# The first layer's MLP in two passes: the context, then the latents in units with seven products for eight

## The chip, the core and the metric

One core of a Trainium2 chip runs the whole kernel. The time is device microseconds (us) of one execution; the metric is the median over runs. TensorE (PE) does the matrix products and has a queue for weight loads of its own (PEld). VectorE (DVE), ScalarE (ACT) and GpSimd (POOL) do the elementwise work, and SyncE (SP) issues the DMA transfers.

## The reference, cut to what matters

```python
def _mlp(h, w1, w2):                       # D_MODEL 1024, hidden 4096
    return jnp.square(jax.nn.relu(h @ w1)) @ w2

for i in range(2):                         # layer 0: conv/Fourier mixer; layer 1: neighbourhood attention
    sx1, cx1, gx1, sx2, cx2, gx2 = split(cond_x @ ada_w[i] + ada_b[i])   # for the latents
    sc1, cc1, gc1, sc2, cc2, gc2 = split(cond_c @ ada_w[i] + ada_b[i])   # for the context
    x = x + gx1 * mixer_i(modulate(rms(x), sx1, cx1))                    # 1024 latent tokens
    if i == 0: ctx = ctx + gc1 * mixer_0(modulate(rms(ctx), sc1, cc1))   # 256 context tokens
    x = x + gx2 * _mlp(modulate(rms(x), sx2, cx2), w1[i], w2[i])
    if i == 0: ctx = ctx + gc2 * _mlp(modulate(rms(ctx), sc2, cc2), w1[i], w2[i])
return x
```

In layer 1 the context gives keys and values, so that `ctx` is needed for its norm and its part of K and V, and no longer after that. All data are fp32.

## The kernel before

**Tokens and numbers.** Tokens lie along the free axis, channels along the 128 partitions. They are cut into chunk 0 and chunk 1 (512 latent tokens each) and chunk 2 (256 context tokens). Every operand of a product is held as a high and a low part, and a product is three matmuls into one PSUM bank: high by high, high by low, low by high (`mm3`, lines 298 to 300). A group of matmuls ends in PSUM; `residual` (line 315, DVE) scales it by the gate and adds it to the tokens' tile `xT`, which frees the bank. There are eight banks.

**Weights.** 512 KB of weights come into a tile `raw` (three of them, tag `wraw`) by one DMA of SP's queue. Each half becomes a piece `wsp` (four of them): ACT copies the high part (line 251), and POOL, or in places DVE, subtracts to get the low part (line 252).

**Layer 0's MLP.** `mlp(0, norm, (2, 1, 0), 0, 1, end0)` walks over eight blocks of 512 hidden channels. In a block four groups of the first product (`up`: ACT line 970 relu and line 972 square, POOL line 973 square again, DVE line 974 low part) run over the chunks 2, 1 and 0 with the same weights; the second product follows in groups over the same chunks, each ended by a `residual`. So 1280 tokens share each piece of weights, and 128 pieces serve the pass.

**Work beside it.** `tick` gives places to `ada_filler`: it takes a step of layer 1's adaLN map, eight reductions on DVE (line 222, two instructions each) of a 512 KB tile. 48 steps are needed; all of them stand beside this pass. At its start chunk 0's norm stands between the products (`norm.stat`, then `norm.out` per 128 channels: lines 404 to 412 on DVE, ACT and POOL). At its end `end0` puts the squares of the next norm (line 377) behind the residuals, and chunk 0's norm ahead of the last groups.

**After it.** The products of Q, K and V (lines 1163 and 1164) take the chunks as token tiles of 128: tiles 0 to 3 are chunk 0, 4 to 7 chunk 1, 8 and 9 the context. The first weight kind begins with chunk 0, then takes the context, then chunk 1. Layer 1's MLP does part of the work here described as units (`unit_head`, `unit_tail`, `unit_down`): 256 hidden channels, 2 by 2 blocks of the first product formed with seven products of sums for eight (Strassen's way, in Winograd's form). Sums of the tokens (`token_sums`, `token_sum_3`, `token_sum_4`: lines 1383 to 1411) and of the weights (`make_s2`) are made on DVE and POOL for that.

A scheduler ahead of time decides how the instructions of one engine stand in its queue; each engine runs its queue in order. The functions of the kernel that the change touches are these.

Of the kernel before, what the change touches and what calls it, by code (L numbers as in the profile page):

```python
# [36 lines left out]
def trunk(ctx: ExitStack, tc, x_t, cx_t, vecs, cc, ada, ada_t, w_in, w_out_2, w_fold, w_32, mlp_w1, mlp_w2, w_qkv, na_w_out_2, na_w_out_4, bias_pad,  # L37
# [916 lines left out]
    gs = partial_groups(y_hi[2:4], y_lo[2:4], 0, 0, (0,), 2, done=lambda m, ci: norm.square(m, ci, POOL if m % 2 else DVE))  # L954
    close_stream(gs[:4], gs[4:], (1,), norm)


    def mlp(l, norm, cis, late, fill, end, nf=8, beside=()):


        beside = list(beside)
        hh, hl = norm.hi, norm.lo

        def up(pcs, ci, uh, ul, between=None):
            off, w, _ = CHUNKS[ci]
            ps = dense(pcs, ci, hh, hl)
            if between:
                between()
            r, q = tmp(), tmp()
            ACT.activation(r[:, :w], ps[:, :w], AF.Relu)  # L970
            hs = uh[:, off:off + w]
            ACT.activation(hs, r[:, :w], AF.Square)
            POOL.tensor_tensor(out=q[:, :w], in0=r[:, :w], in1=r[:, :w], op=ALU.mult)  # L973
            DVE.tensor_tensor(out=ul[:, off:off + w], in0=q[:, :w], in1=hs.bitcast(F32), op=ALU.subtract)  # L974

        order = [ci for ci in cis if ci != late] + [late]
        for fc in range(nf):
            uh = [big("uh") for _ in range(4)]
            ul = [big("ul") for _ in range(4)]
            f = 0  # L980
            if fc == 0:
                pcs = take()
                pcs += [w for a in plan.pop(0) for w in pieces(*a, lambda: big("wq")[:, 0:1024])]
                for n, ci in enumerate(order):
                    for i in range(3):
# [4 lines left out]
                        else:  # L990
                            up(w, ci, uh[i], ul[i])
                            if beside and (ci, i) > (late, 0):
                                beside.pop(0)()
                f = 3
            while f < 4:
                pcs = take()
                for ci in order:
                    up(pcs, ci, uh[f], ul[f])
                    if beside:
                        beside.pop(0)()  # L1000
# [695 lines left out]
```

## Time and profile before

| what | value |
|---|---|
| median of three runs | 2715.81 us (2714.42 to 2718.0) |
| the profiled execution's own time | 2716.18 us |
| its span in the trace | 2714.4 us |
| PE busy | 2631.4 us, 97% |
| DVE busy | 1682.5 us, 62% |
| ACT busy | 914.5 us, 34% |
| POOL busy | 1029.1 us, 38% |

The span is the time from the first to the last instruction that the profiler shows. Busy shares are means over stages that have different limits, so the stretches are read one by one. A matmul's busy time overlaps the next one's, so that the rate at which PE works is read from starts, or from the count of matmuls in a stretch.

### The profile page before, as it was taken

The page shows a single profiled execution, that of the slowest core. Times are in us where ns is not written, and L with a number is a line of the kernel's source. Part 1 is how long each engine was busy: PE and PEld are TensorE (multiplying, and loading weights), DVE is VectorE, ACT ScalarE, POOL GpSimd, SP SyncE. Part 2 cuts the span into 40 slices and gives each one's busy share as a digit, 9 for nine tenths or more (in the row PEclk, how much of TensorE's full clock was granted, in tenths as well). Part 3 has the DMA queues.
Part 4 walks back from the last instruction along what each step waited for, and adds up shares of the span by engine and source line. Part 5 has one row for each costly group of instructions (what it writes and reads, how often), then busy time and mean ns, then how long its engine had stood idle before and what let it go on. Part 6 is the DMA issues. An engine that isn't in the chain of part 4 may idle for free. (4 is left out here: it accounts for less than half of the span.)

```text
span 2714.4 us, 37385 instructions
## 1 busy us (share of the span) xinstructions
PE 2631.4 (97%) x13787; PEld 2186.2 (81%) x13787; DVE 1682.5 (62%) x3635; ACT 914.5 (34%) x1988; POOL 1029.1 (38%) x850
## 2 busy tenths in 40 slices
PE   7999898999999999999999999999999999999999
PEld 5878787888888888888778887788877788888887
DVE  5798678454465555623962544888879855555555
ACT  4211246121221211213532324766754232332332
POOL 3232347232332322323410102444457644544543
PEclk8999899999999999999999999999999999999999
DMA  7244320222222222311333444434321111111112
GB/s 249 72 132 130 124 75 16 68 88 82 82 94 69 86 90 78 94 47 43 101 115 107 122 130 143 148 105 143 104 59 39 47 47 47 63 47 47 63 47 86
DMA packets 150395, 239.46 MB, mean 88 GB/s; under 512 B 10892, under 2 KB 94124, under 8 KB 150212
## 3 DMA queue, kind: packets, MB, share of 16 engines
q1 hardware_dynamic: 148772, 234.45, 27.2%
q8 instruction: 109, 1.79, 0.3%
q10 hardware_dynamic: 1440, 2.62, 0.3%
q14 instruction: 74, 0.61, 0.1%
HBM read 208.71 MB, written 28.32 MB: 87 GB/s over the span
## 5 line engine op out<-in xcount | busy, mean ns | idle before, releaser
L252 POOL TENSOR_TENSOR wsp<-raw,wsp 128x512 fp32r<-128x512 f32 x355 | 498.4, 1407 | 898.6 <-ACT wsp L251 871.1
L315 DVE SCALAR_TENSOR_TENSOR xT<-ps,mods,xT 128x512 f32<-128x512 f32 x544 | 380.7, 711 | 316.8 <-PE ps L300 316.2
L298 PE MATMUL ps<-uh,wsp 128*128 128x512 f32 (+1 forms) x1280 | 471.2, 369 | 10.5 <-DVE xT L315 10.5
L299 PE MATMUL ps<-ul,wsp 128*128 128x512 f32 (+1 forms) x1280 | 471.7, 369 | 0.6 <-DVE ul L1505 0.6
L300 PE MATMUL ps<-uh,wsp 128*128 128x512 f32 (+1 forms) x1280 | 470.6, 368 | 0.0
L222 DVE CUSTOM_DVE_ANT_0 junk<-raw,cond_b 128x256 bf16<-128x256 f32 x640 | 346.3, 541 | 198.9 <-DMA raw<-in_ada_t_dram 167.3
L251 ACT CAST wsp<-raw 128x512 fp32r<-128x512 f32 x368 | 226.1, 619 | 716.2 <-PE ps L300 540.6
L299 PE MATMUL ps<-ml,wsp 128*128 128x512 f32 (+1 forms) x792 | 285.4, 361 | 9.7 <-DVE ml L412 7.5
L298 PEld LDWEIGHTS ps<-uh,wsp 128*128 128x128 f32 x1280 | 241.3, 188 | 55.1 <-DVE xT L315 10.8
L298 PE MATMUL ps<-mh,wsp 128*128 128x512 f32 (+1 forms) x792 | 283.9, 360 | 1.2 <-ACT mh L405 1.2
L300 PE MATMUL ps<-mh,wsp 128*128 128x512 f32 (+1 forms) x792 | 283.6, 359 | 0.0
L299 PEld LDWEIGHTS ps<-ul,wsp 128*128 128x128 f32 x1280 | 241.3, 189 | 41.0 <-DVE ul L1505 1.1
L300 PEld LDWEIGHTS ps<-uh,wsp 128*128 128x128 f32 x1280 | 241.0, 188 | 40.6
L973 POOL TENSOR_TENSOR tmp<-tmp 128x512 f32<-128x512 f32 (+1 forms) x104 | 103.3, 994 | 217.1 <-ACT tmp L970 148.2
L299 PEld LDWEIGHTS ps<-ml,wsp 128*128 128x128 f32 x792 | 150.9, 191 | 36.5 <-DVE ml L412 10.9
L298 PEld LDWEIGHTS ps<-mh,wsp 128*128 128x128 f32 x792 | 150.9, 191 | 24.6 <-ACT mh L405 1.4
L300 PEld LDWEIGHTS ps<-mh,wsp 128*128 128x128 f32 x792 | 151.0, 191 | 21.3
L1499 PE MATMUL ps<-mh,wsp 128*128 128x512 f32 x448 | 142.6, 389 | 0.0
L970 ACT ACTIVATE tmp<-ps 128x512 f32<-128x512 f32 (+1 forms) x104 | 55.3, 531 | 255.5 <-PE ps L300 250.8
L298 PE MATMUL ps<-hh,wsp 128*128 128x512 f32 (+1 forms) x360 | 130.1, 361 | 3.9 <-ACT wsp L251 3.6
L974 DVE TENSOR_TENSOR ul<-tmp,uh 128x512 fp32r<-128x512 f32 (+1 forms) x104 | 92.4, 893 | 66.5 <-POOL tmp L973 66.5
L299 PE MATMUL ps<-hl,wsp 128*128 128x512 f32 (+1 forms) x360 | 129.4, 359 | 2.0 <-DVE hl L412 1.4
(335 smaller groups left out, 5098.5 us busy)
## 6 DMA issues: line engine op xcount, KB each, us to landing
raw<-in_mlp_w_dram SPq DMA_DIRECT2D x96, 512.0 KB, 3.5
raw<-in_ada_t_dram SPq DMA_DIRECT2D x80, 512.0 KB, 3.8
raw<-in_mlp_w_dram SPq DMA_DIRECT2D x72, 256.0 KB, 2.7
raw<-in_w_qkv_dram SPq DMA_DIRECT2D x24, 512.0 KB, 4.1
k_d<-tmp SPq DMA_DIRECT2D x40, 256.0 KB, 2.4
kh<-k_d SPq DMA_DIRECT2D x15, 640.0 KB, 5.0
kl<-k_d SPq DMA_DIRECT2D x15, 640.0 KB, 7.3
araw<-in_ada_dram SPq DMA_DIRECT2D x16, 512.0 KB, 9.4
```

Source lines behind the costliest of these rows:

```text
L222: DVE.tensor_tensor_reduce(out=junk, in0=raw[:, d * 256:d * 256 + 256], in1=cond_b, op0=ALU.mult, op1=ALU.add, scale=1.0, scalar=0.0, accu ...
L251: ACT.copy(dst_hi, src)
L252: lo_eng.tensor_tensor(out=dst_lo, in0=src, in1=dst_hi.bitcast(F32), op=ALU.subtract)
L298: PE.matmul(ps, lhsT=whi, rhs=ahi, start=first, stop=False)
L299: PE.matmul(ps, lhsT=whi, rhs=alo, start=False, stop=False)
L300: PE.matmul(ps, lhsT=wlo, rhs=ahi, start=False, stop=last)
L315: DVE.scalar_tensor_tensor(out=xT[dt][ci], in0=ps, scalar=mods[l][:, 24 * k + 16 + dt, s:s + 1], in1=xT[dt][ci], op0=ALU.mult, op1=ALU.add)
L970: ACT.activation(r[:, :w], ps[:, :w], AF.Relu)
L973: POOL.tensor_tensor(out=q[:, :w], in0=r[:, :w], in1=r[:, :w], op=ALU.mult)
L974: DVE.tensor_tensor(out=ul[:, off:off + w], in0=q[:, :w], in1=hs.bitcast(F32), op=ALU.subtract)
L1499: PE.matmul(ps, lhsT=a, rhs=b, start=(first and kt == 0 and n == 0), stop=(kt == 3 and n == 2), skip_group_check=True)
```

## The change

Layer 0's MLP becomes two passes. The first is the context alone: 64 tiles `raw`, 128 pieces, and twelve matmuls of 256 columns with each piece. Every third piece is split on DVE, the others on POOL. Beside it stand the norms of chunks 1 and 0 and the sums of the latents (`sums_12`, `sum_3`, near the end `sum_4`). The context is then saved to DRAM and its tile is reused. The second pass is the latents: the class `Seven`, which also takes the place of layer 1's code, runs over 16 units of 256 hidden channels. The weights are so loaded and split a second time, with sums of the weights (`make_s2`) in every unit. In the first 14 units two adaLN steps stand beside the second product; the other 20 go beside Q, K and V, where none stood before. The last unit's second product goes chunk by chunk (with its weights made twice), and the first kind of QKV begins with the context's tiles 8 and 9.

```diff
-    def plan_mlp(l, n=8):
...
-    plan_mlp(0)
...
-    fillers.extend([ada_filler] * 49)
-    mlp(0, norm, (2, 1, 0), 0, 1, end0)
...
+    def ctx_make(ahead_):
+        while w_at[0] < 128 and len(w_made) < ahead_:
+            n, k = divmod(w_at[0], 2)
+            if k == 0:
+                ctx_raw()
+            w = wp.tile([P, 1024], F32R, tag="wsp", name="wsp")
+            split_act(w[:, 0:512], w[:, 512:1024], w_raw[n][:, 512 * k:512 * k + 512], DVE if w_at[0] % 3 == 1 else POOL)
+            w_made.append(w)
+            w_at[0] += 1
...
+    class Seven:
...
+        def product(self, ps, bs, first):
+            w = self.next_w()
+            for kt, (bh, bl) in enumerate(bs):
+                wh, wl = w[:, kt * P:kt * P + P], w[:, 512 + kt * P:512 + kt * P + P]
+                for n, (a, b) in enumerate(((wh, bh), (wh, bl), (wl, bh))):
+                    for p, cs in ((b, H0),) if not isinstance(b, tuple) else zip(b, (slice(0, 256), slice(256, 512))):
+                        PE.matmul(ps[:, cs], lhsT=a, rhs=p, start=(first and kt == 0 and n == 0), stop=(kt == 3 and n == 2),
+                                  skip_group_check=True)
...
+        def tail(self, i, head):
+            a, s1 = head
+            us = self.room(i)
+            b, c, u2, u3 = bank(), bank(), keep(), keep()
+            part = lambda n, cs: (us[n][0][:, cs], us[n][1][:, cs])
+            self.product(b, self.t["t2"], True)
+            DVE.tensor_tensor(out=u2, in0=b, in1=s1, op=ALU.add)
+            self.product(a, self.quarter(upper, H0), False)
+            squared(tmp(), *part(0, H0), a)
+            self.product(b, self.quarter(lower, H1), False)
+            DVE.tensor_tensor(out=u3, in0=b, in1=s1, op=ALU.add)
+            self.product(c, self.t["t1"], True)
...
+    for ci in (1, 0):
+        beside0.append(lambda ci=ci: norm.stat(ci))
+        for dt in range(DT):
+            beside0 += [lambda dt=dt, ci=ci: norm.out(dt, ci)] + [None] * (2 - ci)
+    for kt in range(4):
+        beside0 += s0.sums_12(kt, s0_t1[kt], halves(wide[kt]), keep)
+    for kt in range(4):
+        beside0 += s0.sum_3(kt, keep)
...
+    for fc in range(8):
+        uh, ul = wide[0:4], wide[4:8]
+        for f in range(4):
+            ps = dense([ctx_w()], 2, m_hi, m_lo, (0, 4))
+            dense([None, ctx_w()], 2, m_hi, m_lo, (4, 8), ps)
...
+            ACT.activation(r, ps[:, :w2], AF.Relu)
+            ACT.activation(uh[f][:, F0], r, AF.Square)
+            ACT.activation(q, r, AF.Square)
+            DVE.tensor_tensor(out=ul[f][:, F0], in0=q, in1=uh[f][:, F0].bitcast(F32), op=ALU.subtract)
+            beside_step()
+        for m in range(DT):
+            w = ctx_w()
+            ps = bank()[:, :w2]
+            for q in range(4):
+                mm3(ps, w[:, P * q:P * q + P], w[:, 512 + P * q:512 + P * q + P], uh[q][:, F0], ul[q][:, F0], q == 0, q == 3)
+            residual(ps, m, 2, 0, 1)
+            beside_step()
...
+    def between0(i, us):
+        steps = [lambda: None] * 4 + [ada_issue, lambda: (ada_step(), ada_issue()), lambda: None, ada_step]
+        s0.down(us, None, steps if i < 14 else ())
...
+    s0.run(last0)
+    fillers.extend([ada_filler] * 21)
...
-        tiles = [0, 1, 2, 3] + ([] if kind == 0 else [8, 9]) + [4, 5, 6, 7]
+        tiles = [8, 9, 0, 1, 2, 3, 4, 5, 6, 7] if n == 0 else [0, 1, 2, 3] + ([] if kind == 0 else [8, 9]) + [4, 5, 6, 7]
...
-            tick()
+            tick(n == 2 or n < 5 and i > 3 and i % 2 == 0 or 0 < n < 5 and i % 2 == 0)
```

Of the seven products of a unit the one with the sums `t4`, and the one with `t1` for two of its four channel blocks, find their operand in two tiles of 256 columns, so that these 18 matmuls of 512 columns are issued as 36 of 256. A unit's first product then has 66 matmuls of 512 and 36 of 256 columns, and its second product 96 of 512.

Three places show how the queues change. The first is POOL's queue in the MLP's first third. Before, it holds splits of weights (line 252, of a tile `raw`) and the activation's square (line 973).

```order
L973 TENSOR_TENSOR tmp_4622<-tmp_4621 128x512
L252 TENSOR_TENSOR wsp_4672<-raw_4670,wsp_4672 128x512
L973 TENSOR_TENSOR tmp_4655<-tmp_4654 128x512
L252 TENSOR_TENSOR wsp_4675<-raw_4670,wsp_4675 128x512
L973 TENSOR_TENSOR tmp_4704<-tmp_4703 128x256
L973 TENSOR_TENSOR tmp_4735<-tmp_4734 128x512
L252 TENSOR_TENSOR wsp_4797<-raw_4795,wsp_4797 128x512
```

Now, in the context's pass, it holds splits (line 253 of the changed kernel), the norm's products for chunk 0 (line 412; `xT0` is chunk 0's token tile) and sums of the latents' high and low parts (line 985).

```order
L253 TENSOR_TENSOR wsp_4339<-raw_4234,wsp_4339 128x512
L253 TENSOR_TENSOR wsp_4357<-raw_4280,wsp_4357 128x512
L985 TENSOR_TENSOR ny_4927<-mh0_2947,ml0_2955 128x512
L412 TENSOR_TENSOR tmp_4377<-xT0_84,ny_4273 128x512
L253 TENSOR_TENSOR wsp_4400<-raw_4320,wsp_4400 128x512
L985 TENSOR_TENSOR ny_4968<-mh4_2951,ml4_2959 128x512
L253 TENSOR_TENSOR wsp_4420<-raw_4320,wsp_4420 128x512
L253 TENSOR_TENSOR wsp_4458<-raw_4355,wsp_4458 128x512
L985 TENSOR_TENSOR ny_5089<-mh1_2948,ml1_2956 128x512
L412 TENSOR_TENSOR tmp_4553<-xT0_84,ny_4273 128x512
L253 TENSOR_TENSOR wsp_4476<-raw_4398,wsp_4476 128x512
```

The square is ACT's now, and parts of norm and sums stand between the splits, by which the pieces are made. The second place is DVE's queue in a block's products. Before, the eight reductions of an adaLN step (line 222) stood between the low parts of the first product (line 974).

```order
L974 TENSOR_TENSOR ul_5427<-tmp_5788,uh_5423 128x512
L222 ISA junk_106,parts_107<-raw_5928,cond_b_5885 128x256
L222 ISA parts_107 128x1
L222 ISA junk_106,parts_107<-raw_5928,cond_b_5885 128x256
L222 ISA parts_107 128x1
L230 TENSOR_TENSOR parts_107<-parts_107 128x32
L974 TENSOR_TENSOR ul_5428<-tmp_5839,uh_5424 128x256
```

Now, at the end of a unit, the reductions (line 223) stand between the residuals (line 316).

```order
L316 SCALAR_TENSOR_TENSOR xT1_85<-ps_7260,mods0_75,xT1_85 128x512
L223 ISA junk_106,parts_107<-raw_7242,cond_b_6953 128x256
L223 ISA parts_107 128x1
L223 ISA junk_106,parts_107<-raw_7242,cond_b_6953 128x256
L223 ISA parts_107 128x1
L316 SCALAR_TENSOR_TENSOR xT1_85<-ps_7268,mods0_75,xT1_85 128x512
L1119 TENSOR_TENSOR ny_7290<-ps_7288,ny_7116 128x512
L1123 TENSOR_TENSOR ny_7291<-ps_7288,ny_7116 128x512
```

A bank of the second product is freed behind up to two reductions, and the next unit's first addition (line 1119) stands behind the last residual. The third place is DVE's queue at the change to Q, K and V, where the last residuals of chunk 1 (`xT1`) meet the norm for layer 1. Before, norm, residuals and splits stand there.

```order
L412 TENSOR_TENSOR al7_10278<-tmp_10744,ah7_10270 128x512
L315 SCALAR_TENSOR_TENSOR xT1_85<-ps_10783,mods0_75,xT1_85 128x512
L252 TENSOR_TENSOR wq_10821<-raw_10819,wq_10821 128x512
L377 TENSOR_TENSOR ny_10613<-ny_10613,tmp_10780 128x512
L390 TENSOR_SCALAR tmp_10862<-ps_10860 128x256
L252 TENSOR_TENSOR wq_10829<-raw_10827,wq_10829 128x512
L377 TENSOR_TENSOR ny_10613<-ny_10613,tmp_10797 128x512
```

Now the context's norm has been done by then, chunk 0's stands there (lines 358 to 360 and 405; `xT2_11258` holds its sum of squares), and reductions of the adaLN steps stand in it.

```order
L316 SCALAR_TENSOR_TENSOR xT1_85<-ps_11674,mods0_75,xT1_85 128x512
L253 TENSOR_TENSOR wq_11719<-raw_11717,wq_11719 128x512
L391 TENSOR_SCALAR tmp_11652<-ps_11650 128x512
L378 TENSOR_TENSOR xT2_11258<-xT2_11258,tmp_11636 128x512
L358 SCALAR_TENSOR_TENSOR tmp_11653<-xT2_11258 128x512
L223 ISA junk_106,parts_107<-raw_11963,cond_b_10941 128x256
L223 ISA parts_107 128x1
L359 TENSOR_TENSOR tmp_11653<-tmp_11653,tmp_11652 128x512
L223 ISA junk_106,parts_107<-raw_11963,cond_b_10941 128x256
L223 ISA parts_107 128x1
L378 TENSOR_TENSOR xT2_11258<-xT2_11258,tmp_11667 128x512
L360 SCALAR_TENSOR_TENSOR xT2_11258<-tmp_11653,xT2_11258 128x512
```

From there to the last part of chunk 1's norm 31 such reductions stand in DVE's queue, where before there was none.

## Rows read from the trace of the kernel before

**Rows 1.** The page, part 1: busy time, share of the span, instructions.

```profile
PE 2631.4 (97%) x13787; PEld 2186.2 (81%) x13787; DVE 1682.5 (62%) x3635; ACT 914.5 (34%) x1988; POOL 1029.1 (38%) x850
```

**Rows 2.** Stretches: length, busy (xcount) of PE, PEld, DVE, ACT, POOL; PEclk, DMA.

```profile
500.00:1200.00 700.00, 700.00 (x3655) 603.06 (x3654) 369.27 (x1022) 135.99 (x245) 205.84 (x174) 1.00 0.26 83
2200.00:2600.00 400.00, 400.00 (x1767) 331.20 (x1766) 220.21 (x285) 116.21 (x192) 186.85 (x146) 1.00 0.16 52
```

**Rows 3.** PE's timeline in layer 0's MLP, 256 columns: start, duration, instruction.

```profile
760.71 0.28 PE L298 MATMUL ps<-uh,wsp 128*128 128x256 f32 x1
...
762.14 0.40 PE L298 MATMUL ps<-uh,wsp 128*128 128x512 f32 x1
```

**Rows 4.** One stretch, as rows 2: chunk 0's norm at the MLP's start.

```profile
430.00:450.00 20.00, 12.99 (x52) 9.55 (x51) 17.84 (x18) 12.02 (x21) 14.19 (x10) 0.74 0.10 27
```

**Rows 5.** DVE's groups, 500 to 1290: busy us, mean ns, idle before.

```profile
L222 DVE CUSTOM_DVE_ANT_0 junk<-raw,cond_b 128x256 bf16<-128x256 f32 x384 | 211.1, 550 | 156.0 <-DMA raw<-in_ada_t_dram 146.4
L315 DVE SCALAR_TENSOR_TENSOR xT<-ps,mods,xT 128x512 f32<-128x512 f32 x117 | 87.5, 749 | 145.3 <-PE ps L300 145.0
...
L222 DVE DVE_READ_ACCUMULATOR2_ANT parts<- 128x1 f32 x384 | 30.9, 81 | 0.0
L315 DVE SCALAR_TENSOR_TENSOR xT<-ps,mods,xT 128x256 f32<-128x256 f32 x61 | 29.4, 482 | 41.4 <-PE ps L300 41.4
L974 DVE TENSOR_TENSOR ul<-tmp,uh 128x256 fp32r<-128x256 f32 x28 | 14.3, 510 | 7.8 <-POOL tmp L973 7.8
```

**Rows 6.** POOL's groups, the same stretch.

```profile
L252 POOL TENSOR_TENSOR wsp<-raw,wsp 128x512 fp32r<-128x512 f32 x118 | 159.1, 1348 | 365.0 <-ACT wsp L251 353.2 <-DVE xT L315 5.6 <-DVE parts L222 3.2
L973 POOL TENSOR_TENSOR tmp<-tmp 128x512 f32<-128x512 f32 x56 | 60.0, 1072 | 154.8 <-ACT tmp L970 121.0 <-DVE ul L974 22.3 <-DVE parts L230 9.9
```

**Rows 7.** ACT's groups, the same stretch.

```profile
L251 ACT CAST wsp<-raw 128x512 fp32r<-128x512 f32 x117 | 72.5, 619 | 383.8 <-PE ps L300 383.8
...
L972 ACT ACTIVATE uh<-tmp 128x256 fp32r<-128x256 f32 x28 | 11.7, 418 | 0.9
```

**Rows 8.** DVE's groups, 2040 to 2140: layer 1's sums.

```profile
L1383 DVE TENSOR_TENSOR tmp<-mh,ml 128x512 f32<-128x512 f32 x8 | 11.0, 1371 | 0.1
...
L252 DVE TENSOR_TENSOR ml<-tmp,mh 128x512 fp32r<-128x512 f32 x4 | 4.9, 1221 | 0.0
```

**Rows 9.** POOL's groups, the same stretch.

```profile
L1383 POOL TENSOR_TENSOR tmp<-mh,ml 128x512 f32<-128x512 f32 x16 | 25.9, 1628 | 1.3 <-DVE ol L252 0.6 <-DVE ml L252 0.6
L252 POOL TENSOR_TENSOR wsp<-raw,wsp 128x512 fp32r<-128x512 f32 x13 | 20.8, 1598 | 2.6 <-ACT wsp L251 2.6
```

**Rows 10.** The stretch of those sums, as rows 2.

```profile
2090.00:2140.00 50.00, 39.51 (x164) 29.71 (x163) 49.59 (x55) 12.07 (x22) 41.27 (x28) 1.00 0.11 32
```

**Rows 11.** DVE's timeline in it: start, duration, instruction.

```profile
2099.72 0.67 DVE L1383 TENSOR_TENSOR tmp<-mh,ml 128x512 f32<-128x512 f32 x1
2100.32 1.78 DVE L1395 TENSOR_TENSOR tmp<-tmp 128x512 f32<-128x512 f32 x1
```

**Rows 12.** The page, part 6: a DMA of weights, us from issue to landing.

```profile
raw<-in_mlp_w_dram SPq DMA_DIRECT2D x96, 512.0 KB, 3.5
```

**Rows 13.** DVE's groups, 1300 to 1400: the change to Q, K and V.

```profile
L404 DVE SCALAR_TENSOR_TENSOR tmp<-xT,g,ny 128x512 f32<-128x512 f32 x8 | 9.6, 1207 | 0.1
L377 DVE TENSOR_TENSOR ny<-ny,tmp 128x512 f32<-128x512 f32 x7 | 9.1, 1306 | 0.1
L252 DVE TENSOR_TENSOR wq<-raw,wq 128x512 fp32r<-128x512 f32 x6 | 7.3, 1210 | 0.2 <-ACT wq L251 0.2
L412 DVE TENSOR_TENSOR al<-tmp,ah 128x512 fp32r<-128x512 f32 x8 | 7.0, 870 | 0.0
...
L406 DVE SCALAR_TENSOR_TENSOR al<-tmp,mods,ah 128x512 fp32r<-128x512 f32 x8 | 5.9, 741 | 0.7 <-ACT ah L405 0.7
```

**Rows 14.** One stretch, as rows 2: the change to Q, K and V.

```profile
1320.00:1370.00 50.00, 40.26 (x172) 31.12 (x172) 47.22 (x81) 30.18 (x59) 21.27 (x15) 0.97 0.30 95
```

**Rows 15.** One stretch, as rows 2: Q, K and V.

```profile
1400.00:1600.00 200.00, 200.00 (x929) 165.42 (x928) 85.11 (x185) 55.92 (x112) 19.86 (x14) 1.00 0.36 113
```

More of the change, by code (lines that the diff above doesn't have):

```diff
@@ L952, in close_stream @@
             t()
[L954 to L985, printed above, removed]
-                        w = pcs[2 * i:2 * i + 2]
-                        if (n, i) == (1 - l, 0):
-                            up(w, ci, uh[i], ul[i], lambda: norm.stat(late))
-                            norm.all_out(late)
[L990 to L1000, printed above, removed]
-                    tick(fill and fc and ci < 2)
-                f += 1
-            if fc < nf - 1:
-                for g in partial_groups(uh, ul, l, 1, order, 4):
-                    g()
-                    tick()
-            else:
-                flush()
-                end(uh, ul)
@@ new lines, in trunk, with whole, parts_of @@
+    ctx_make(2)
+    H0, H1 = slice(0, 512), slice(512, 1024)
+    F0 = slice(NLAT, NTOK)
+    lower, upper = range(0, 4), range(4, 8)
+    def whole(hl, eng, t):
+        eng.tensor_tensor(out=t, in0=hl[0].bitcast(F32), in1=hl[1].bitcast(F32), op=ALU.add)
+        return t
+    def parts_of(dst, src, eng):
+        for hi, lo, cs in (((dst[0], dst[1], H0),) if not isinstance(dst[0], tuple)
+                           else zip(dst[0], dst[1], (slice(0, 256), slice(256, 512)))):
+            split_act(hi, lo, src[:, cs], eng)
@@ L1501, in squared @@
-    def squared(r, uh, ul, cs, src):
-        ACT.activation(r, src, AF.Relu)
-        ACT.activation(uh[:, cs], r, AF.Square)
-        POOL.tensor_tensor(out=r, in0=r, in1=r, op=ALU.mult)
-        DVE.tensor_tensor(out=ul[:, cs], in0=r, in1=uh[:, cs].bitcast(F32), op=ALU.subtract)
-    def added(ps, s):
-        c = tmp()
-        DVE.tensor_tensor(out=c, in0=ps, in1=s, op=ALU.add)
-        return c
-    def unit_head(i):
-        a = bank()
-        product(a, quarter(lower, H0), True)
-        s1 = keep()
-        ACT.copy(s1, a)
-        return a, s1
@@ new lines, in trunk, with up, beside_up @@
+    hh, hl = m_hi, m_lo
+    def up(pcs, ci, uh, ul, between=None):
+        off, w, _ = CHUNKS[ci]
+        ps = dense(pcs, ci, hh, hl)
+        if between:
+            between()
+        cs = slice(off, off + w)
+        squared(tmp(), uh[:, cs], ul[:, cs], ps)
+    def beside_up(kt):
+        if kt > 1:
+            s1.down_raw(0, kt - 2)
+        for f in s1.sums_12(kt, *(halves(op_.tile([P, NLAT], F32R, tag=g, name=g)) for g in ("oh", "ol"))):
+            f()
+    uh = [big("uh") for _ in range(4)]
@@ L1558, in store @@
+    pcs = take()
+    for ci in range(2):
+        up(pcs, ci, uh[3], ul[3])
+        beside_up(2 + ci)
     def store(m, ci):
```

446 lines of the change are left out of this document (267 added, 179 removed).

## The prediction

> **What bounds the kernel now.** I read the page first: PE is busy for 97% of the span [rows 1], so a gain must come from fewer matmuls or from the few gaps. Then I read the stretches. In layer 0's MLP and in layer 1's units PE is busy all the time at the full clock of 2.4 GHz [rows 2]. The second of these stretches has 1767 matmuls of 512 columns in 400 us, 0.2264 us each. With 256 columns twelve matmuls start between 760.71 and 762.14, 0.1192 us each [rows 3]. So two halves cost 5% more than one whole. The gaps stand at stage changes. When chunk 0's norm runs at the start of the MLP, PE issues 52 matmuls in 20 us, worth 52 x 0.2264 = 11.8; 8.2 us are lost [rows 4]. Inside the MLP the helpers wait: DVE for PE and for adaLN's tiles [rows 5], POOL for ACT [rows 6], ACT for PE [rows 7]. That cover is what the change draws on. Where DVE and POOL make layer 1's sums together, their operations cost more: a sum takes 1.37 on DVE and 1.63 on POOL [rows 8, 9], a split on POOL 1.60 instead of 1.35 [rows 6, 9]. PE is busy for 39.51 of 50 us there, 79%, with DVE full and POOL at 83% [rows 10].
>
> **Matmuls removed.** A unit of 256 channels needs 84 matmuls' worth of 512 columns for 96 in its first product; its second product keeps 96. Sixteen units save 16 x 12 x 0.2264 = 43.5 us. Of the 84, 18 (all of t4's, half of t1's) are issued as two halves: 16 x 18 x (2 x 0.1192 - 0.2264) = 3.5 us. Balance -40.0. The context's 1536 matmuls cost the same 183 us as before.
>
> **The first gap.** Norms of chunks 1 and 0 now run beside the context's matmuls, a pass ahead of their use: -8.2, if PE does not wait for them elsewhere, which is the next term.
>
> **The context's pass.** PE has twelve matmuls of 256 columns per piece, 1.43 us, where before a piece served 1280 tokens. So each piece now has to be ready within a fifth of the time. 85 of the 128 splits are POOL's, with 36 norm products and sums. At the light prices [rows 6] this is 85 x 1.35 + 36 x 1.07 = 153 of 183 us; at the dear ones [rows 9] it is 121 x 1.6 = 194, 11 too many. DVE has 64 residuals, 55 splits, 32 low parts, norms and sums: about 122 us at light prices [rows 5] and 170 at dear ones [rows 8]. ACT has 128 casts at 0.62 and 96 short ones at 0.42, 120 us, and some 25 for norms and sums [rows 7]; it is not the bound, but it leads each split. The beside work is crowded into the first two thirds: before a run of 31 splits in a row, POOL has 52 splits and 28 others, 128 us at 1.6 against PE's 78 x 1.43 = 112, 16 late. DVE's queue added up in the same way is about 20 late near piece 61. At light prices neither is over 3 late. Since both engines do sums of two tiles at the same time, but residuals and waits lie between, I take half way, 9. At the end the last sums (two POOL and three DVE operations, four times) stand behind the last splits: 5. ACT's start: 3. Together +17, bounds +3 and, at PE's share in rows 10, 183 / 0.79 - 183 = +49. The sums' cost shows one by one in the trace: a DVE sum of 0.67 us and behind it one of 1.78 while POOL reads [rows 11]. The Trainium skill ("SBUF — State Buffer", section "Who interferes with whom") says that a DVE instruction with two SBUF inputs contends with a GpSimd instruction that reads SBUF, and that the loser fully blocks; the pair of 0.67 and 1.78 agrees. Were every such operation of the pass to exclude the other engine's, POOL's 153 and some 75 us of DVE's would stand in one row, 228 us for PE's 183, +45: that is rival A. DMA does not bound: a load lands in 3.5 us [rows 12], one is needed each 2.86, and three are in flight.
>
> **The units.** As layer 1's units they take DVE for 55% and POOL for 47% [rows 2]. Two adaLN steps add 16 x (0.55 + 0.08) = 10.1 us [rows 5] to a unit of about 41 us: DVE 81%. The steps stand between residuals, one or two at a time, so a bank is freed about 1.3 us later and the additions that the next product needs come behind. Eight banks cover this; +2 for 14 units, bounds 0 and +10. The second load and split of all weights, and `make_s2`, I cost at nothing: rows 2 show the same work with PE full. If that cover is gone, a unit loses what a late piece costs, 1.4 us. Saving and reloading the context lie beside 15 units.
>
> **The change to Q, K and V.** DVE's queue from the last unit's first residual to chunk 1's last low part: 16 residuals at 0.74 are 12 us, 14 additions of squares 16 [rows 13], outs of three norms 35, three stats 7, six splits 7, the first tiles' Q and K norms 13, and 31 adaLN reductions 20 [rows 5]. That is 110, and 99 when the overlap of some 0.07 us between neighbours [rows 11] is taken off 150 instructions. PE's work ahead of the last low part is 96 matmuls of the second product and 165 to 228 of QKV, 59 to 74 us, since it takes chunk 1's tiles together, block by block. So PE runs dry for 25 to 40 us; some reductions and Q and K norms of that queue fall into waits, so I take the low end, 26. Before, the same place had 172 matmuls in 50 us, 11 us lost [rows 14]. So +15, bounds 0 (if reductions fall into waits) and +30 (dear prices all the way). The other adaLN steps of QKV, some 85 us of DVE, I cost at nothing: DVE is busy for 85 of 200 us there [rows 15]. Without that cover they would delay the Q and K norms, which free banks, by 0.6 us a reduction.
>
> **Sum.** -40.0 - 8.2 + 17 + 2 + 15 = -14.2, from the profiled execution's own 2716.18: 2702 us. The median is 0.4 lower, which I leave out.
>
> **The rivals.** A, on the other side: DVE and POOL hold each other up through the whole context's pass, as at 79% in rows 10. Then the pass costs +49 instead of +17: 2734. It decides once the pass loses over 31 us. For it speaks that both queues are over 90% full at dear prices; against it, that a run of 31 splits at the end lets POOL catch up. B: the helpers keep up (pass +5) and the change to Q, K and V is no worse than before (0): 2675. The waits of rows 5 to 7 speak for it. C: only the adaLN reductions at dear prices fall wholly on PE at the change (+30): 2717. D: the gaps of the pass drop PE's clock to 1.2 GHz, as the mean of 0.74 in rows 4 shows for 20 us with 7 of them idle; 40 us of that would cost 20 more, and 2722 with the rest as forecast. Against it: rows 10 have a full clock with 10.5 of 50 us idle, in shorter gaps.
>
> **How the numbers follow.** A measurement of this kernel can tell about 0.2%, 5.4 us. Forecast (2692 to 2710) 0.40, B 0.20, C 0.15, A 0.18, D 0.07. Faster by more than 0.2% (under 2710.4): forecast and B, 0.60. Slower (over 2721.2): A, and most of D, 0.24. Within: C and the rest, 0.16. The range reaches from B to a little past A's 2734: 2675 to 2738. The part of A beyond that (if each piece waits on each sum), and times below B, are the 2 in 10 left out.
>
> **What would show it.** From 420 on the context's pass should take about 200 us: PE 90% busy, POOL over 85%, its splits between 1.35 and 1.6, with PE's waits put down to POOL's and DVE's splits. The units should have 443 matmuls' worth of 512 columns per 100 us and no gap over 1 us. The change to Q, K and V should show PE idle for some 26 us, waiting for DVE's `al`. The forecast is wrong if the pass takes over 215 us, if units wait for residuals, or if PE's clock falls for long.

## The result, and the profile after

The changed kernel takes 2776.89 us and the kernel before 2716.2, each the median of four runs. The ratio is 1.0221, with an interval of 1.0204 to 1.0239. It is slower by 61 us where 14 less were forecast. The first view is the page's part 1, which answers to [rows 1].

```profile
PE 2624.0 (95%) x13883; PEld 2179.2 (79%) x13883; DVE 1952.0 (70%) x3986; ACT 1041.8 (38%) x2232; POOL 1236.3 (45%) x975
```

PE has 7 us less to do and stands idle for 68 us more. DVE, POOL and ACT have all gained work: 270, 207 and 127 us. The next view is of stretches, as [rows 2, 4, 10, 14]: the context's pass up to the end of the sums beside it, the rest of the pass, the change to the units, the units from the first one's second product to the 15th's, the last unit, and Q, K and V.

```profile
423.30:580.00 156.70, 129.10 (x947) 121.37 (x946) 143.62 (x153) 89.48 (x182) 122.00 (x80) 0.95 0.43 131
580.00:652.60 72.60, 70.88 (x576) 69.31 (x575) 36.52 (x55) 40.58 (x89) 48.02 (x36) 1.00 0.53 168
652.60:688.00 35.40, 29.08 (x140) 23.65 (x140) 18.58 (x26) 15.48 (x32) 25.34 (x20) 0.90 0.29 102
688.00:1294.70 606.70, 598.58 (x2867) 502.66 (x2866) 436.56 (x884) 171.37 (x285) 282.76 (x215) 1.00 0.25 79
1294.70:1343.40 48.70, 42.57 (x190) 34.76 (x190) 34.80 (x51) 25.71 (x49) 27.62 (x21) 0.93 0.24 75
1343.40:1708.70 365.30, 336.87 (x1501) 272.24 (x1501) 225.53 (x661) 112.65 (x219) 52.05 (x39) 0.97 0.45 136
```

In the first row PE issues 947 matmuls of 256 columns in 156.7 us; 947 x 0.1192 is 113, so 44 are lost, with DVE busy for 92% of the time. In the second, where only splits and the context's own work are left, 576 matmuls in 72.6 us are almost the full rate. The whole table of losses, each stage against its matmuls at 0.2264 and 0.1192 us, is as follows. Its edges lie up to 0.7 us off a stage's first matmul.

| stage | took, us | worth, us | lost | the same before |
|---|---|---|---|---|
| context's pass, 423.3 to 652.6 | 229.3 | 183.1 | 46.2 | |
| change to the units, to 688.0 | 35.4 | 22.0 | 13.4 | |
| units, to 1294.7 | 606.7 | 595.2 | 11.5 | |
| last unit, to 1343.4 | 48.7 | 38.2 | 10.5 | |
| layer 0's MLP together | 920.1 | 838.5 | 81.6 | 895.6 for 878.6: 17.0 lost |
| Q, K and V, to 1708.7 | 365.3 | | | 337.2 |
| all after it | 1066.3 | | | 1057.1 |

A unit is worth 96 x 0.2264 in its second product and 66 x 0.2264 + 36 x 0.1192 in its first. So the MLP is 24.5 us longer, Q, K and V 28.1 and the rest 9.2; with 1.2 gained ahead of it these are the 60.6 us between the spans. What the kernel before lost in its MLP, it lost nearly all at the start and nothing at the end, as two of its stretches show.

```profile
424.50:460.00 35.50, 28.49 (x140) 23.20 (x139) 30.50 (x32) 18.87 (x34) 22.75 (x17) 0.86 0.07 21
1290.00:1320.10 30.10, 30.10 (x144) 25.03 (x143) 27.04 (x31) 15.51 (x27) 15.00 (x10) 1.00 0.28 88
```

The view of waits from 423 to 580 tells who is waited for in the pass (engine and line, the one waited for: us, times, longest).

```profile
PE ps L301 <- DVE wsp L253: 13.1, 11, 2.4
...
PE ps L301 <- POOL wsp L253: 5.8, 6, 1.8
...
PE ps L300 <- DVE w L1278: 4.6, 4, 1.5
```

PE waits for low parts of weights that DVE makes, though DVE makes only one in three, then for POOL's, then for the low part of the activation (line 1278). What these operations take is in DVE's and POOL's groups of the pass, 423 to 652, which answer to [rows 5 to 9].

```profile
L253 DVE TENSOR_TENSOR wsp<-raw,wsp 128x512 fp32r<-128x512 f32 x41 | 44.2, 1078 | 12.6 <-ACT wsp L252 12.5
L1278 DVE TENSOR_TENSOR w<-tmp,w 128x256 fp32r<-128x256 f32 x32 | 31.9, 998 | 17.8 <-ACT tmp L1277 17.8
L316 DVE SCALAR_TENSOR_TENSOR xT<-ps,mods,xT 128x256 f32<-128x256 f32 x60 | 27.3, 477 | 15.7 <-PE ps L301 15.7
...
L985 DVE TENSOR_TENSOR ny<-mh,ml 128x512 f32<-128x512 f32 x8 | 11.1, 1384 | 0.0
```

```profile
L253 POOL TENSOR_TENSOR wsp<-raw,wsp 128x512 fp32r<-128x512 f32 x84 | 125.2, 1503 | 43.5 <-ACT wsp L252 40.2 <-issue 2.3 <-DVE tmp L405 0.6
L985 POOL TENSOR_TENSOR ny<-mh,ml 128x512 f32<-128x512 f32 x12 | 18.0, 1499 | 11.5 <-DVE ny L1201 7.0 <-DVE w L253 2.5 <-DVE ml L413 1.2
```

The residual, with an input in PSUM, takes 0.48 as before. DVE's operations on two tiles of SBUF are dear: the low part of 256 columns went from 0.51 to 1.0, a split takes 1.08 and a sum 1.38 (0.45, 0.74 and 0.68 in a run below without POOL beside them).

### The profile page after: what moved, and what is told of

The parts are those of the page before. It is cut to its first block, busy times and chain, and to the rows that moved or that the text cites. A ratio compares the mean times of both kernels' runs of the same rounds, so it can differ in the third digit from the quotient of the medians.

```text
span 2775.0 us, 38416 instructions
## 1 busy us (share of the span) xinstructions
PE 2624.0 (95%) x13883; PEld 2179.2 (79%) x13883; DVE 1952.0 (70%) x3986; ACT 1041.8 (38%) x2232; POOL 1236.3 (45%) x975
## 5 line engine op out<-in xcount | busy, mean ns | idle before, releaser
L253 POOL TENSOR_TENSOR wsp<-raw,wsp 128x512 fp32r<-128x512 f32 x454 | 644.3, 1424 | 782.7 <-ACT wsp L252 761.3
L316 DVE SCALAR_TENSOR_TENSOR xT<-ps,mods,xT 128x512 f32<-128x512 f32 (+1 forms) x672 | 470.5, 715 | 149.7 <-PE ps L301 148.9
L1103 PE MATMUL ps<-mh,wsp 128*128 128x512 f32 (+1 forms) x1216 | 349.6, 368 | 8.1 <-DVE ny L1119 6.3
L1103 PEld LDWEIGHTS ps<-mh,wsp 128*128 128x128 f32 x1216 | 215.8, 189 | 49.3 <-ACT tmp L1003 4.4
L299 PE MATMUL ps<-uh,wsp 128*128 128x512 f32 x528 | 208.2, 394 | 8.8 <-DVE xT L316 6.7
L300 PE MATMUL ps<-ul,wsp 128*128 128x512 f32 x528 | 206.7, 391 | 1.2 <-DVE ul L1006 1.2
L301 PE MATMUL ps<-uh,wsp 128*128 128x512 f32 x528 | 206.6, 391 | 0.0
L301 PE MATMUL ps<-w,wsp 128*128 128x256 f32 (+1 forms) x512 | 172.4, 345 | 10.8 <-DVE wsp L253 8.6
L300 PE MATMUL ps<-w,wsp 128*128 128x256 f32 (+1 forms) x512 | 173.6, 342 | 4.6 <-DVE w L1278 4.6
L299 PE MATMUL ps<-w,wsp 128*128 128x256 f32 (+1 forms) x512 | 173.1, 345 | 4.3 <-ACT wsp L252 3.0
L1010 DVE TENSOR_TENSOR tmp<-ps,ny 128x512 f32<-128x512 f32 x90 | 62.2, 691 | 126.4 <-PE ps L1103 124.4
L1005 POOL TENSOR_TENSOR tmp<-tmp 128x512 f32<-128x512 f32 x128 | 141.2, 1104 | 8.7 <-ACT uh L1004 6.7
L299 PE MATMUL ps<-hh,wsp 128*128 128x512 f32 (+1 forms) x360 | 130.4, 362 | 4.3 <-ACT wsp L252 3.9
L301 PE MATMUL ps<-hh,wsp 128*128 128x512 f32 (+1 forms) x360 | 128.3, 357 | 1.5 <-POOL wsp L253 1.5
L299 PEld LDWEIGHTS ps<-uh,wsp 128*128 128x128 f32 x528 | 99.8, 189 | 35.8 <-DVE xT L316 7.3
```

The costliest lines, as they stand in the source:

```text
L253: lo_eng.tensor_tensor(out=dst_lo, in0=src, in1=dst_hi.bitcast(F32), op=ALU.subtract)
L299: PE.matmul(ps, lhsT=whi, rhs=ahi, start=first, stop=False)
L300: PE.matmul(ps, lhsT=whi, rhs=alo, start=False, stop=False)
L301: PE.matmul(ps, lhsT=wlo, rhs=ahi, start=False, stop=last)
L316: DVE.scalar_tensor_tensor(out=xT[dt][ci], in0=ps, scalar=mods[l][:, 24 * k + 16 + dt, s:s + 1], in1=xT[dt][ci], op0=ALU.mult, op1=ALU.add)
L1005: POOL.tensor_tensor(out=r, in0=r, in1=r, op=ALU.mult)
```

## The experiments

Pass, units and Q, K and V below are timed in the trace of each run as in the table above. Totals stand beside the 2776.9 of the changed kernel. A stage whose code is the same differs by up to 2 us from run to run: the pass takes 228.8 to 231.0 in the five runs that leave it as it is.

**Without the adaLN steps beside Q, K and V.** The 20 steps are left out, and the modulation of layer 1's MLP is zero.

```diff
-    fillers.extend([ada_filler] * 21)
+    POOL.memset(mods[1][:, 24:48, :], 0.0)
+    POOL.memset(gtile[1][1], 0.0)
```

> The changed kernel without the 20 adaLN steps beside Q, K and V (left out; the modulation of layer 1's MLP is set to zero). Theory 1 (the steps cost PE there, since norms and weight splits stand behind them in DVE's queue and some wait for their DMA): the stretch of Q, K and V falls from 365 us to about 340, the total from 2777 to about 2750. Rival (the reversed order of tiles and the norms alone cost it): the stretch stays above 358, the total above 2770.

Measured: 2742.4 us, Q, K and V 342.4. The steps cost 22.9 us there; without them the stretch is 5 us longer than before. The total fell by 34.5, 7.7 of it in the attention behind, which has no such steps (more on that below).

**The kernel before with those steps moved.** This is the one part alone.

```diff
-    fillers.extend([ada_filler] * 49)
+    fillers.extend([ada_filler] * 29)
     mlp(0, norm, (2, 1, 0), 0, 1, end0)
+    fillers.extend([ada_filler] * 20)
...
-            tick()
+            tick(n == 2 or n < 5 and i > 3 and i % 2 == 0 or 0 < n < 5 and i % 2 == 0)
```

> The kernel before with only the placing of adaLN changed: 29 steps stay beside layer 0's MLP, 19 go beside Q, K and V with the changed kernel's rule of ticks. Theory 1 (steps there cost PE): the stretch of Q, K and V grows from 337 us to about 357, the total from 2716 to about 2736. Rival (they are free, as 43% of DVE is busy there): the total stays under 2722.

Measured: 2739.0 us, ratio 1.0085 (1.0056 to 1.0115); Q, K and V 358.4 instead of 337.2, 21.2 more. So most of the loss comes with the steps and not with the order of the tiles. The view of stretches shows the three runs, Q, K and V of the run without the steps, of before, and of before with the steps.

```profile
1337.80:1680.20 342.40, 332.58 (x1500) 271.21 (x1500) 170.16 (x331) 114.10 (x218) 54.32 (x39) 0.98 0.35 109
```

```profile
1320.10:1657.30 337.20, 327.46 (x1502) 268.89 (x1501) 164.35 (x333) 112.48 (x220) 50.39 (x37) 0.99 0.36 113
```

```profile
1320.20:1678.60 358.40, 335.58 (x1503) 273.85 (x1502) 218.78 (x647) 111.55 (x220) 49.06 (x37) 0.97 0.45 140
```

With the steps DVE is busy for 54 us more than before and has idle time left in the mean, but PE loses 21. How this comes about is seen in the changed kernel's waits from 1343 to 1600.

```profile
DVE junk L223 <- DMA raw<-in_ada_t_dram: 32.0, 11, 6.7
...
PE ps L1467 <- DVE wsp L253: 8.0, 3, 5.0
...
PE ps L1468 <- DVE al L407: 4.9, 3, 2.8
PE ps L1468 <- DVE al L413: 4.7, 3, 2.0
...
PE ps L102 <- DVE ny L1504: 4.0, 4, 1.7
```

DVE stands still for 32 us in front of reductions whose tile hasn't landed. Behind them in its queue are weight splits for the next kind, the low parts `al` of the norm and the Q and K norms, and for each of these PE waits. SP's own waits, 1480 to 1560, close the circle: the load of QKV weights (line 1338) waits for a buffer that an adaLN tile holds until DVE has read it.

```profile
SPq L1338 <- DVE parts L231: 4.0, 1, 4.0
SPq L1338 <- DMA raw<-in_ada_t_dram: 3.1, 1, 3.1
SPq L1338 <- DVE parts L223: 2.8, 1, 2.8
```

**Without the sums beside the context's pass.** `sums_12` and `sum_3` are left out; 16 copies by ACT stand for their results.

```diff
-        beside0 += s0.sums_12(kt, s0_t1[kt], halves(wide[kt]), keep)
-    for kt in range(4):
-        beside0 += s0.sum_3(kt, keep)
+        s0.t.setdefault("t1", []).append(s0_t1[kt])
+        s0.t.setdefault("t2", []).append(halves(wide[kt]))
+        beside0 += [lambda q=q: ACT.copy(q, x_all[0][:, 0, :]) for q in (*s0_t1[kt], *halves(wide[kt]))]
```

> The changed kernel without the sums sums_12 and sum_3 beside the context's pass (left out; 16 copies by ACT, one per step, stand in for their results). Theory 1 (DVE and POOL, dearer by doing two-tile operations at the same time, are late with the pieces): the pass from its first matmul to the first product of a unit falls from 229 us to about 210, the total to about 2757. Rival (the pieces themselves, two thirds POOL's, are the limit): the pass stays above 222.

Measured: 2745.2 us, pass 203.5. The sums cost the pass 25.8 us, more than half of what it loses.

**All splits on POOL.**

```diff
-            split_act(w[:, 0:512], w[:, 512:1024], w_raw[n][:, 512 * k:512 * k + 512], DVE if w_at[0] % 3 == 1 else POOL)
+            split_act(w[:, 0:512], w[:, 512:1024], w_raw[n][:, 512 * k:512 * k + 512], POOL)
```

> The changed kernel with every one of the 128 splits of the context's pass on POOL. If PE waits above all because DVE's queue holds its 43 splits behind other work, the pass gets shorter than 229 us, to about 220. If POOL's and DVE's common price is what counts, POOL has 128 x 1.45 + 36 x 1.5 = 240 us of work and the pass takes about 240, the total about 2788.

Measured: 2782.8 us, pass 237.1. DVE was freed of a third of the splits, and the pass got longer. But POOL is now busy for 228.9 of the 237.1 us and is the limit itself, so this run doesn't tell how much DVE's queue alone held the pass up; two runs further on do.

**The price by itself.** A small kernel stands in place of the model, in a single execution: it forms one product, runs 24 operations of each phase and writes a tile to the output; the model itself is left out.

```diff
+    add = lambda eng, c=512: lambda o, g: eng.tensor_tensor(out=o[:, 0:c], in0=g[:, 0:c], in1=w[:, 0:c], op=ALU.subtract)
+    res = lambda c=512: lambda o, g: DVE.scalar_tensor_tensor(out=o[:, 0:c], in0=bank[:, 0:c], scalar=w[:, 0:1], in1=g[:, 0:c], op0=ALU.mult, op1=ALU.add)
...
+    phase("alone", dve=add(DVE))
+    phase("palone", pool=add(POOL))
+    phase("both", dve=add(DVE), pool=add(POOL))
+    phase("half", dve=add(DVE, 256), pool=add(POOL))
+    phase("psum", dve=res(), pool=add(POOL))
+    phase("stt", dve=ada_, pool=add(POOL))
```

> Not the model but the prices by themselves: 24 operations of 128x512 each, on DVE alone, on POOL alone, on both at once, and on both with DVE at 256 columns or with one of DVE's inputs in PSUM. Theory (a two-tile operation of DVE and one of POOL exclude each other): alone DVE takes 0.67 and POOL 1.25 to 1.3 us; at once each DVE operation takes about 1.3 to 1.9 us, with 256 columns hardly less, and with an input in PSUM 0.74 as alone. Rival (they share a rate): at once DVE takes 0.8 to 1.0, POOL 1.5, and 256 columns halve it.

The groups of that run, by phase, first DVE's and then POOL's:

```profile
L66 DVE SCALAR_TENSOR_TENSOR stt_dve<-g_stt,w 128x512 f32<-128x512 f32 x24 | 40.2, 1750 | 14.3 <-ACT g_stt L54 14.3
L63 DVE TENSOR_TENSOR both_dve<-g_both,w 128x512 f32<-128x512 f32 x24 | 39.0, 1701 | 31.1 <-ACT g_both L54 31.1
L63 DVE TENSOR_TENSOR half_dve<-g_half,w 128x256 f32<-128x256 f32 x24 | 32.6, 1433 | 2.5 <-ACT g_half L54 2.5
L64 DVE SCALAR_TENSOR_TENSOR psum_dve<-bank,w,g_psum 128x512 f32<-128x512 f32 x24 | 15.9, 742 | 2.5 <-ACT g_psum L54 2.5
L63 DVE TENSOR_TENSOR alone_dve<-g_alone,w 128x512 f32<-128x512 f32 x24 | 14.5, 683 | 6.9 <-ACT g_alone L54 6.9
```

```profile
L63 POOL TENSOR_TENSOR both_pool<-g_both,w 128x512 f32<-128x512 f32 x24 | 40.1, 1706 | 0.8 <-ACT g_both L54 0.8
...
L63 POOL TENSOR_TENSOR half_pool<-g_half,w 128x512 f32<-128x512 f32 x24 | 33.7, 1439 | 1.4 <-ACT g_half L54 1.4
L63 POOL TENSOR_TENSOR psum_pool<-g_psum,w 128x512 f32<-128x512 f32 x24 | 29.4, 1268 | 1.4 <-ACT g_psum L54 1.4
L63 POOL TENSOR_TENSOR palone_pool<-g_palone,w 128x512 f32<-128x512 f32 x24 | 29.3, 1262 | 21.9 <-ACT g_palone L54 21.9
```

Alone DVE takes 0.68 and POOL 1.26. At once both take 1.70, and 24 pairs need 40 us, 1.67 a pair, where one after the other they would need 0.60 + 1.22 = 1.82 (14.5 / 24 and 29.3 / 24). So they take turns, but for a small overlap. With 256 columns DVE's operation still takes 1.43, about as long as POOL's whole one beside it. The rival, a shared rate, is out: by it the half width would have halved the time. Both engines read the same tiles here; in the pass they mostly read different ones, and their operations are dear there as well. With one input in PSUM nothing is lost, 0.74 and 1.27. This agrees with the Trainium skill ("SBUF — State Buffer", section "Who interferes with whom"), by which a DVE instruction with at most one SBUF input, outside DVE's two-port modes, does not contend with GpSimd, and one with two contends with a GpSimd instruction that reads SBUF, under an exclusive lock.

**All splits on DVE, and POOL out of the pass.** In the first run `DVE` stands for the choice in the splits' line above. In the second the norms' products and the sums go to DVE as well (`sum_3` as `sums_12`).

```diff
-        def sums_12(self, kt, t1, t2, room=tmp):
+        def sums_12(self, kt, t1, t2, room=tmp, POOL=POOL):
...
-            beside0 += [lambda dt=dt, ci=ci: norm.out(dt, ci)] + [None] * (2 - ci)
+            beside0 += [lambda dt=dt, ci=ci: norm.out(dt, ci, True)] + [None] * (2 - ci)
...
-        beside0 += s0.sums_12(kt, s0_t1[kt], halves(wide[kt]), keep)
+        beside0 += s0.sums_12(kt, s0_t1[kt], halves(wide[kt]), keep, DVE)
...
```

> The changed kernel with all 128 splits of the context's pass on DVE, nothing else changed. Theory (a two-tile operation of DVE and one of POOL exclude each other, 0.6 against 1.22 us): the pass held 85 x 1.22 of POOL's splits and now holds 85 x 0.6 more on DVE, so the row of excluding work falls by 50 us, to some 165 of 183; the pass takes about 200 us instead of 229, the total is about 2750. Rival (PE waits because DVE's queue is full in order): DVE gets 51 us more work, the pass takes 245 or more, the total is above 2790.

> As the run with all splits on DVE, with the norms' products and the sums beside the pass (but the four last sums) on DVE too, so that POOL is hardly used there. Theory: nothing excludes DVE any more, but it has some 175 us of work for 183: the pass takes 195 to 205 us, about as the run before it. Rival (what is left on POOL costs still): 10 us shorter than that run.

Measured: 2763.4 us with a pass of 215.8, and 2749.9 us (ratio 1.0131, 1.0111 to 1.0151) with a pass of 207.2. DVE got 85 splits more, and then 24 further operations of POOL's, and each time the pass became shorter, by 13.5 and 22.1 us in all. That is the theory's side, with half of the size that was expected of the first step; what POOL kept there cost 8.6 more, as the second run's rival had it. The view shows the pass with all splits on POOL, with all on DVE, and without POOL.

```profile
421.60:658.70 237.10, 205.33 (x1522) 191.74 (x1522) 163.01 (x167) 132.47 (x272) 228.94 (x158) 0.96 0.45 140
```

```profile
423.50:639.30 215.80, 201.17 (x1531) 191.98 (x1530) 188.23 (x294) 129.84 (x272) 59.74 (x35) 0.97 0.50 154
```

```profile
421.60:628.80 207.20, 198.79 (x1532) 191.46 (x1531) 184.19 (x320) 125.37 (x264) 16.46 (x12) 0.97 0.50 161
```

DVE's groups of the pass without POOL:

```profile
L253 DVE TENSOR_TENSOR wsp<-raw,wsp 128x512 fp32r<-128x512 f32 x126 | 91.2, 738 | 15.6 <-ACT wsp L252 14.0
...
L1278 DVE TENSOR_TENSOR w<-tmp,w 128x256 fp32r<-128x256 f32 x32 | 14.5, 454 | 0.0
L985 DVE TENSOR_TENSOR ny<-mh,ml 128x512 f32<-128x512 f32 x20 | 13.5, 682 | 0.0
```

A split takes 0.74 instead of 1.08, the low part 0.45 instead of 1.0 and a sum 0.68 instead of 1.38. 24 us of the loss are left. DVE is busy for 184 of the 207 us there, and the granted clock of 0.97 is worth up to 207 x 0.03 = 6 of the 24; what sets the rest was not tried. Nor was a fifth or sixth buffer for the pieces, which might cover part of these waits. The same 20 steps beside Q, K and V cost more in these runs than in the changed kernel: that stretch takes 373 and 368 us instead of 365.

**No adaLN step at all.** All 48 are left out, and layer 1's modulation is zero.

```diff
...
-        s0.down(us, None, steps if i < 14 else ())
+        s0.down(us)
...
-    fillers.extend([ada_filler] * 21)
```

> The changed kernel without any of layer 1's 48 adaLN steps (left out; its modulation is zero). Theory: the small gaps in the units (9 us over 15 units) go too, since the reductions stand ahead of the additions that the next product waits for; the total falls to about 2732, 10 below the run that left out the 20 steps beside Q, K and V. Rival (the gaps are of other waits): no more than 2 us below it.

Measured: 2736.9 us. The units take 596.1 us for a worth of 595.2, as the view shows.

```profile
689.20:1285.30 596.10, 596.10 (x2867) 503.81 (x2866) 327.52 (x426) 172.56 (x285) 275.69 (x215) 1.00 0.15 51
```

So the seven products give all that they promise when nothing stands beside them. The steps cost the units 10.6 us against the changed kernel and 7.3 against the run without the 20 others (603.4). The total fell by only 5.5 against that run, between the theory's 10 and the rival's 2, because what stands ahead of the units, the same in both, took 3.4 us longer. The waits of the changed kernel in the units say where it goes, from 700 to 1290:

```profile
PE ps L1103 <- DVE ny L1119: 6.3, 5, 1.6
```

It is the first addition (line 1119), which stands behind residuals and reductions in the second of the queues shown with the change.

**Both left out.** The 20 steps and the sums beside the pass.

> The changed kernel without the 20 adaLN steps beside Q, K and V and without the sums beside the context's pass (both left out). Theory: the two losses are separate, so they add: 2777 - 34 - 32 = 2711, that is 5 below before. Rival (one hides in the other): 2725 or more.

Measured: 2722.1 us, ratio 1.0025 (1.0014 to 1.0036), 11 above the sum of the single effects. About eight of them were counted twice: the attention takes 326.0 us in the changed kernel, but 318.3, 319.7 and 319.9 in the runs without the steps, without the sums and without both. The pass is 205.4 and Q, K and V 342.3, as in the single runs. So the losses of pass and QKV are separate, and without both the kernel would still not beat the one before.

**The steps placed otherwise.** First three steps in each of the first eight units and 10 beside Q, K and V; then two in all units and 18 there. In both they are meant to stand only in a kind's first tiles, a kind being one of the six groups of weights of Q, K and V.

```diff
-        steps = [lambda: None] * 4 + [ada_issue, lambda: (ada_step(), ada_issue()), lambda: None, ada_step]
-        s0.down(us, None, steps if i < 14 else ())
+        no, go = lambda: None, lambda: (ada_step(), ada_issue())
+        steps = [no, no, ada_issue, go, no, go, no, ada_step] if i < 8 else [no] * 4 + [ada_issue, go, no, ada_step]
+        s0.down(us, None, steps)
...
+    places = {1: (0, 1, 3), 2: (0, 1, 3, 5), 3: (0, 1, 3, 5), 4: (0, 1, 3)}
+    for at in places.values():
+        fillers.extend([ada_issue] + [go] * (len(at) - 2) + [ada_step])
...
+            tick(i in places.get(n, ()))
```

In the second run `steps` are the changed kernel's for every unit, and the places are these:

```diff
+    places = {1: range(5), 2: range(7), 3: range(5), 4: range(5)}
```

> The changed kernel with the steps placed otherwise, nothing left out: three in each of the first 8 units, two in the others, 10 beside Q, K and V, and there only in a weight kind's first tiles, so that none holds a buffer of raw weights when the next kind's weights are loaded. Theory (what costs is the queue behind a step that waits for its tile, and the buffer it holds): Q, K and V take about 348 us instead of 365, the units lose 5 more, the total is about 2763. Rival (DVE's time as such costs): no gain in Q, K and V beyond half of it, and the units lose 10 or more, total 2775 or above.

> The changed kernel with the adaLN steps placed otherwise: two in the 15th unit as well, and 18 beside Q, K and V, only in the first tiles of four weight kinds and not in the first or last kind, so that no step holds a buffer of raw weights when a kind's weights are loaded and none stands in the norms of the first kind. Theory: Q, K and V take about 347 us instead of 365 with the units as before, the total is about 2757. Rival (DVE's time as such): less than 8 us gained.

Measured: 2803.7 us for the first. Q, K and V fell to 346.1, as expected, but the units grew from 606.7 to 659.2: a third step costs 6.6 us a unit, where the two together had cost 0.8. There the casts of weights wait for raw tiles, 66.5 us from 700 to 1000 where the changed kernel has 24.1, and the loads of the second product's weights (line 1047) wait for reductions and adaLN's tiles, which hold the buffers:

```profile
ACT wsp L252 <- DMA raw<-in_mlp_w_dram: 66.5, 11, 8.8
...
PE ps L1103 <- DVE ny L1123: 17.0, 6, 4.3
```

```profile
SPq L1047 <- DVE parts L223: 14.4, 3, 4.8
SPq L1047 <- DMA raw<-in_ada_t_dram: 11.8, 3, 4.7
```

The second took 2771.1 us, and Q, K and V 361.0, a gain of 4.3 and within the rival's 8: the theory that the buffers alone do it fails. One of the three places of loss, at the change to the fourth kind, is gone (0.9 instead of 7.4 us within 96 matmuls there); the others stay, since the scheduler had pulled 20 of the reductions ahead of the end of chunk 1's norm again. With 0, 10, 18 and 20 steps the stretch takes 342, 346, 361 and 365 us, but the number alone does not explain it, as the first four of the six kinds show (a step is eight reductions; the last two kinds take 47.4 and 56.6 us in every run).

| run | reductions in kinds 1 to 4 | us of kinds 1 to 4 |
|---|---|---|
| before | none | 72.1, 47.4, 55.5, 58.2 |
| without the 20 steps | none | 77.1, 47.4, 55.5, 58.2 |
| 10 steps | 16, 24, 24, 16 | 80.8, 47.5, 55.5, 58.2 |
| 18 steps | 32, 32, 48, 32 | 84.8, 51.8, 62.2, 58.2 |
| changed, 20 steps | 48, 40, 64, 8 | 84.8, 51.1, 60.4, 64.7 |

In the second and third kind three steps each cost nothing and four to eight cost 4 to 7 us. In the fourth one step within 4 us of its first matmul costs 6.5 us, and four that begin 8 us after it cost nothing, so the place counts too. How much is the late tile and how much the reductions' own time, the runs do not separate.

**Three changes together.** All splits on DVE, the steps as in the last run, and the context's norm in the last unit three groups later (two of its channel blocks are then read after chunk 1's sum of squares has taken their place, so the context's values are others).

```diff
-        todo += [[], [], [lambda: norm1.stat(2)]] + [[lambda d=d: norm1.out(d, 2, True) for d in (2 * k, 2 * k + 1)] for k in range(4)]
-        todo += [[], [], [], [], [lambda: norm1.stat(0)]] + [[lambda d=d: norm1.out(d, 0)] for d in range(2)]
+        todo += [[]] * 5 + [[lambda: norm1.stat(2)]] + [[lambda d=d: norm1.out(d, 2, True) for d in (2 * k, 2 * k + 1)] for k in range(4)]
+        todo += [[], [lambda: norm1.stat(0)]] + [[lambda d=d: norm1.out(d, 0)] for d in range(2)]
```

> All splits of the context's pass on DVE, the adaLN steps as in the run before it, and the context's norm in the last unit three groups later, so that PE doesn't wait there for its sum of squares (5.5 us). If the three gains add: 2777 - 27 - 20 - 5 = 2725; with the attention's first stretch as in the other variants (7 us shorter than in the changed kernel) 2718, about the time of the kernel before. Rival (they hide in each other): above 2735.

Measured: 2743.0 us, ratio 1.0103 (1.0086 to 1.012). The pass kept its gain (215.9) and the attention is 318.1. Q, K and V are at 363.5. PE's wait for the context's sum of squares fell from 5.5 to 2.6 us, but the last unit takes 49.3 us as against 48.7, since PE now waits 2.5 us for its first addition, behind the two steps that stand in the 15th unit. So the steps' new places hardly gained, and what the norm gained was taken back. No version that beats the kernel before was found.

## Why the prediction was wrong

**Matmuls removed: right.** -40.0 was forecast. The units without steps run at their worth, 596.1 for 595.2.

**The context's pass: the right mechanism, the wrong size.** +17 was forecast, 46.2 measured, and 13.4 more at the change to the units, where 5 stood in the sum for the last sums (5.0 are lost there in the run with POOL out of the pass). The step that failed is the choice of the price: "I take half way, 9". The bound of +49 was nearly reached by the pass alone and passed with the change to the units, 59.6 together; rival A, which decides from 31 us on, is what happened. The bound itself was low: it took PE's busy share in [rows 10], 79%, where the count of matmuls gives 164 x 0.2264 = 37.1 of 50 us, 74%, and so +64. Two things were wrong in the working. The dear rows [rows 8, 9] were averages over operations that met and did not meet the other engine; by the price run an operation that meets the other engine's takes 1.4 to 1.7 us, even with half of DVE's columns. And the low part of 256 columns (line 1278) was carried at its light 0.51 in both sums, while it took 1.0. The estimate that lines both engines' two-tile work up in one row, 228 us for PE's 183, came nearest: the pass took 229.3. That it is so near is in part luck: nearly all of the loss lies in the first 157 us, and by the same reckoning the run with all splits on DVE should have taken 200 us and took 215.8.

**The units: +2 forecast, 11.5 measured,** 10.6 of it by the adaLN steps. The prediction saw that the additions come behind and set the banks against it ("Eight banks cover this"); but the next unit's first addition stands behind the last residuals in DVE's queue, and PE waits for it whatever the banks.

**The change to Q, K and V: +15 forecast, about +38 measured** (10.5 lost in the last unit, where PE had no gap before; and 28.1 in Q, K and V). Of these, 10.5 and the 12.7 of the first kind belong to the change itself, 23 us and within the bound of +30; the other 15 lie in the next three kinds. The step that failed there is that "the other adaLN steps of QKV, some 85 us of DVE, I cost at nothing". DVE's mean of 43% [rows 15] was no cover, because DVE's queue is in order: a step whose tile is late stops the splits and norms behind it. In layer 0's MLP the same waits, 146 us [rows 5], had cost nothing [rows 2]; presumably what stood behind them there was not needed for long. Leaving the steps out (-22.9) and moving them alone (+21.2) agree.

**All after it: nothing forecast, +9.2 measured.** About 7 lie in the attention's first 100 us. It takes 326.0 us here and 326 to 327 in the two runs with the pass's work moved to DVE, but 317 to 322 in the nine other runs that have it, one of them with all splits on DVE too, and 319.3 before. The change doesn't touch it; the order of its instructions differs from version to version. Why this order is slower was not tried and stays open.

Rivals B and C did not come about, and no rival let two terms go to their bounds at once: A's pass with C's change would have been 2702 + 32 + 15 = 2749. Of D there is a trace: the granted clock is 0.95 on the mean in the first row of the pass, worth about 157 x 0.05 = 8 of the 44 us lost there. The first gap is gone, as forecast, and it was larger than 8.2 us: 28 of the 52 matmuls in [rows 4] have 256 columns, so they are worth 8.8 us, and 11 of the 20 were lost. The norm that stood there now stands beside the pass.
